# The first convolution of the recurrence between the sums of two norms and their broadcasts

## The chip, the cores and the metric

The kernel runs on one core of a Trainium2 chip. The metric is the device time of one launch in microseconds; the kernel before was run three times. The profile is one execution of the same program.

## What is computed

Four transformer layers over 256 tokens of width 1024. The change concerns the mixers of the last two layers (`_mixer` of the reference). Cut to what matters:

```python
proj = h @ w_in
c_q, c_kv, k_rope, q_m, k_m, v_m, o_m, i_m, f_m, g_mla, g_mlstm = split(proj)
q  = rmsnorm(c_q, q_norm_w) @ w_uq            # 384 -> 8 heads of 96
kv = rmsnorm(c_kv, kv_norm_w) @ w_ukv         # 256 -> 8 heads of 128
y_mla = attention(q, kv, rope(k_rope))
qk = silu(causal_dwconv(concat[q_m, k_m]))    # 4 taps, 1024 channels
y_mlstm = recurrence(qk, v_m, i_m, f_m) * sigmoid(o_m)
out = (sigmoid(g_mla) * (y_mla @ w_br_mla) + sigmoid(g_mlstm) * (y_mlstm @ w_br_mlstm)) @ w_out
```

`c_q` and `c_kv` are the low-rank activations and each has its own norm over its channels. `q_m` (the first 512 channels of `qk`) is what the code calls `conv(0)`.

## The kernel before

Activations lie with channels on the partitions and the 256 tokens along the free axis. Each float32 matrix product is done as three matmuls on halves of the operands: a high part (`wh`, `qH`, `hTh`) and the rest (`wl`, `qL`, `hTl`). So every weight piece of 128x1024 numbers is fetched by a DMA of SP's queue into a buffer `ws` (five), cast on ACT (L260) into `wh` and subtracted on DVE (L261) into `wl`; there are six pairs of `wh` and `wl`. `mm3` then issues the three matmuls (L275 to L277). Some fetches also draw a piece of the conditioning weights after or before them (`tick`), which cost a DMA (L498) and a product on DVE (L499).

The program is written as one long sequence. A scheduler of the framework then lays out each engine's queue: it plays the program through with its own costs, and an engine that is free takes, of the instructions whose operands and buffers are ready, the one that the program wrote first. Each engine then works through its queue in that fixed order. Buffers of one name (the banks `mm` and `acc` in PSUM, four each; `ws`, `wh`, `wl`, `nrm`) are handed out in the order of the program.

In `mixer2` the order of the program around the change is:

- the products `b1` and `b2` give `c_q`, `c_kv` and `k_rope`; copies L1361 to L1367 take them out of PSUM into `Fq`, `Fk`, `kr`
- `pgate`, 24 matmuls for the gates, from a small weight that GpSimd's queue fetches (L1371)
- `chan_norm` for `Fq` (three blocks), then for `Fk` (two): squares on ACT (L1193), sums over channels on TensorE (L1197, rows of the matmul are channels), the scale on DVE (L525) and the power -0.5 on GpSimd (L527), the broadcast over the partitions on TensorE (L554, into a bank `mm`), the product with the weight on DVE (L1201), and the split into `qH` and `qL`, or `vH` and `vL`, on ACT (L299) and DVE (L300)
- the product with `w_uq` in four groups of 18 matmuls, called uq below: own fetches (L1387), casts (L1390 to L1393), copies out (L1399, L1400)
- `conv(0)`: 96 matmuls into two banks `mm`, four activations (L1224), twelve taps on DVE (L1230), and one Silu over all four blocks (L1232)
- the gates' chain of small operations (L1406 to L1429), their transposes (L308), the product with `w_ukv` and the value product `pv` of the recurrence

Of the kernel before, what the change touches and what calls it, by code (L numbers as in the profile page):

```python
# [202 lines left out]
class Kern:  # L203
# [982 lines left out]
        nc.vector.tensor_copy(self.rot["q"][64:96], cs[64:96])  # L1186
        nc.vector.tensor_scalar(self.rot["q"][96:128], sn[96:128], C["sgn_q"][96:128], None, op0=ALU.mult)

    def chan_norm(self, F, n, count, w, H, L):

        nc = self.nc
        sq = self.scr((P, n, S))
        nc.scalar.activation(sq, F, AF.Square)  # L1193
        ps = self.bank("acc")
        for t in range(2):
            for k in range(n):
                nc.tensor.matmul(ps[:, t:t + 1], lhsT=sq[:, k, t * P:(t + 1) * P], rhs=self.one_col,  # L1197
                                 start=(t == 0 and k == 0), stop=(t == 1 and k == n - 1))
        v = self.bcast_rstd(ps[:, 0:2], count)
        for k in range(n):  # L1200
            nc.vector.scalar_tensor_tensor(F[:, k], F[:, k], w[:, k:k + 1], v, op0=ALU.mult, op1=ALU.mult)  # L1201
        self.split(H, L, F)


    def mixer2(self, i, mp, turn):
        nc, A, col = self.nc, self.A, self.col
# [12 lines left out]
        def conv(g):  # L1219
            bs = self.wstat(w_in, 672 + g * 512, 512, hT)  # L1220
            for b in range(2):
                for j in range(2):
                    c = g * 4 + b * 2 + j
                    nc.scalar.activation(mqk[:, c], bs[b][:, j], AF.Identity, bias=cb[:, c:c + 1], scale=cw[:, 24 + c:25 + c])  # L1224
                for j in range(2):
                    c = g * 4 + b * 2 + j
                    x, u = bs[b][:, j], mqk[:, c]
                    for tap in range(3):
                        sft = 3 - tap
                        nc.vector.scalar_tensor_tensor(u[:, sft:], x[:, :S - sft], cw[:, tap * 8 + c:tap * 8 + c + 1],  # L1230
                                                       u[:, sft:], op0=ALU.mult, op1=ALU.add)
            nc.scalar.activation(mqk[:, g * 4:g * 4 + 4], mqk[:, g * 4:g * 4 + 4], AF.Silu)  # L1232
# [126 lines left out]
        Fq, Fk = E4((P, 3, S)), E4((P, 2, S))  # L1359
# [16 lines left out]
        for k in range(KC):  # L1376
            self.mm3(pgate[:40, :S], (gh[:, k], gl[:, k]), (hT[0][:, k], hT[1][:, k]), k == 0, k == KC - 1)

        self.chan_norm(Fq, 3, 384, col["q_norm_w_2", i], qH, qL)
        self.chan_norm(Fk, 2, 256, col["kv_norm_w_2", i], vH, vL)  # L1380


        wu = A["w_uq_2"][i]
        for g in range(4):
# [9 lines left out]
            ps = self.bank("acc", (P, 2, S))  # L1394
# [3 lines left out]
                             hh == 0 and k == 0, hh == 1 and k == 2)  # L1398
            nc.scalar.copy(QH[:64, 2 * g:2 * g + 2], ps[:64])  # L1399
            nc.vector.tensor_tensor(QH[64:, 2 * g:2 * g + 2], ps[64:], self.rot["q"][64:, None, :].to_broadcast([64, 2, S]), ALU.mult)  # L1400
        conv(0)

        G, R = E4((8, 4, S)), E4((8, 4, S))
        ig, lf, Bc, Mx = G[:, 0], G[:, 1], G[:, 2], G[:, 3]
# [25 lines left out]
        ps = self.bank("acc", (P, 2, 4, 8))  # L1430
# [6 lines left out]
        ps = self.bank("acc", (P, 4, 4))  # L1437
# [9 lines left out]
        for g in range(2):  # L1447
            wh, wl = self.wload(A["w_ukv_2"][i].piece(0, g * 512), 2, 512)
            for b in range(2):
                ps = self.bank("acc", (P, 2, S))  # L1450
# [8 lines left out]
            ps = self.bank("acc", (P, 2, S))  # L1459
# [6 lines left out]
        ps = self.bank("acc", (P, 2, S))  # L1466
# [11 lines left out]
        for t in range(2):  # L1478
            v = T((P, 8, 65), f"vx{t}")
# [3 lines left out]
            w = E4((P, 8, 65))  # L1483
# [19 lines left out]
        for t in range(2):  # L1503
            ps = self.bank("acc", (P, 4, P))
# [208 lines left out]
```

## Time and profile before

| | us |
|---|---|
| median of 3 runs | 2158.03 (2157.88 to 2158.73) |
| the profiled execution | 2156.61 |
| its span | 2154.8 |

The span runs from the first to the last profiled instruction, so 1.81 us of the profiled execution lie around it. The two mixers in question lie at about 1300 to 1440 us and 1725 to 1870 us of the span.

### The profile page before, as it was taken

The page shows a single profiled execution, that of the slowest core. Times are in us where ns is not written, and L with a number is a line of the kernel's source. Part 1 is how long each engine was busy: PE and PEld are TensorE (multiplying, and loading weights), DVE is VectorE, ACT ScalarE, POOL GpSimd, SP SyncE. Part 2 cuts the span into 40 slices and gives each one's busy share as a digit, 9 for nine tenths or more (in the row PEclk, how much of TensorE's full clock was granted, in tenths as well). Part 3 has the DMA queues.
Part 4 walks back from the last instruction along what each step waited for, and adds up shares of the span by engine and source line. Part 5 has one row for each costly group of instructions (what it writes and reads, how often), then busy time and mean ns, then how long its engine had stood idle before and what let it go on. Part 6 is the DMA issues. An engine that isn't in the chain of part 4 may idle for free.

```text
span 2154.8 us, 36620 instructions
## 1 busy us (share of the span) xinstructions
PE 2064.4 (96%) x13990; PEld 1892.1 (88%) x13990; DVE 1811.5 (84%) x2593; ACT 1354.7 (63%) x1806; POOL 37.6 (2%) x49
## 2 busy tenths in 40 slices
PE   4999999989999999999999999999999999999998
PEld 4789999787888888888888888899999998989998
DVE  7888888987898999999898987967897878678765
ACT  3555445756878788778777775554655566447553
POOL 0000000000000000000000001000000000000000
PEclk9999999989999999999999999989999999899999
DMA  9768996788999989898999955646587656455662
GB/s 329 254 236 285 341 340 235 248 307 309 351 358 344 362 332 369 287 396 327 353 351 342 348 216 187 224 146 199 200 284 257 222 180 209 146 195 189 224 214 89
DMA packets 161305, 581.03 MB, mean 270 GB/s; under 512 B 17920, under 2 KB 20096, under 8 KB 161120
## 3 DMA queue, kind: packets, MB, share of 16 engines
q1 hardware_dynamic: 160256, 576.42, 74.5%
q8 instruction: 111, 1.82, 0.3%
q10 hardware_dynamic: 720, 1.73, 0.3%
q14 instruction: 74, 0.61, 0.1%
q0 software_dynamic: 144, 0.46, 0.1%
HBM read 577.49 MB, written 1.05 MB: 268 GB/s over the span
## 4 chain that ended last, share of the span: by engine, by line
PE 69%; DVE 4%; issue 2%; ACT 1%; DMA 1%; POOL 1%; DVEq 0%; POOLq 0%; ACTq 0%
PE mm L276 14%; PE mm L275 14%; PE mm L277 14%; PE acc L276 7%; PE acc L275 7%; PE acc L277 7%; DVE wl L261 1%; PE mm L979 1%; PE mm L308 1%; DMA ws<-in_ada_w_dram 1%; PE mm L990 1%; PE acc L308 1%; PE acc L1334 1%; PE acc L1280 1%; PE acc L1251 1%
## 5 line engine op out<-in xcount | busy, mean ns | idle before, releaser
L260 ACT CAST wh<-ws 128x1024 fp32r<-128x1024 f32 x525 | 546.6, 1051 | 421.5 <-PE mm L276 132.7
L261 DVE TENSOR_TENSOR wl<-ws,wh 128x1024 fp32r<-128x1024 f32 x525 | 631.5, 1221 | 102.9 <-ACT wh L260 99.0
L275 PE MATMUL mm<-hTh,wh 128*128 128x256 f32 x1536 | 435.7, 284 | 20.9 <-ACT wh L260 20.1
L277 PE MATMUL mm<-hTh,wl 128*128 128x256 f32 x1536 | 433.9, 283 | 5.3 <-DVE wl L261 5.3
L276 PE MATMUL mm<-hTl,wh 128*128 128x256 f32 x1536 | 434.1, 283 | 0.0
L275 PEld LDWEIGHTS mm<-hTh,wh 128*128 128x128 f32 x1536 | 293.8, 191 | 23.0 <-ACT wh L260 20.4
L277 PEld LDWEIGHTS mm<-hTh,wl 128*128 128x128 f32 x1536 | 293.1, 191 | 6.3 <-DVE wl L261 6.2
L276 PEld LDWEIGHTS mm<-hTl,wh 128*128 128x128 f32 x1536 | 296.9, 193 | 0.4
L275 PE MATMUL mm<-wh,x 128*128 128x512 f32 (+1 forms) x768 | 291.6, 380 | 0.0
L276 PE MATMUL mm<-wl,x 128*128 128x512 f32 (+1 forms) x768 | 288.2, 375 | 1.2 <-DVE wl L261 1.2
L277 PE MATMUL mm<-wh,x 128*128 128x512 f32 (+1 forms) x768 | 286.7, 373 | 0.0
L261 DVE TENSOR_TENSOR wl<-wx,wh 128x1024 fp32r<-128x1024 f32 x219 | 260.7, 1221 | 21.2 <-ACT wh L260 13.8
L499 DVE SCALAR_TENSOR_TENSOR ws<-ws,cb 128x1024 f32<-128x1024 f32 x190 | 230.7, 1220 | 51.0 <-DMA ws<-in_ada_w_dram 48.8
L260 ACT CAST wh<-wx 128x1024 fp32r<-128x1024 f32 x219 | 226.8, 1052 | 51.9 <-PE mm L277 26.2
L275 PE MATMUL acc<-y,wh 128*128 128x256 f32 x736 | 206.5, 283 | 6.5 <-ACT y L303 3.7
L276 PE MATMUL acc<-y,wh 128*128 128x256 f32 x736 | 207.2, 282 | 0.9 <-DVE y L304 0.9
L277 PE MATMUL acc<-y,wl 128*128 128x256 f32 x736 | 207.1, 282 | 0.7 <-DVE wl L261 0.7
L276 PEld LDWEIGHTS mm<-wl,x 128*128 128x128 f32 x768 | 145.6, 190 | 27.9 <-DVE wl L261 4.2
L277 PEld LDWEIGHTS mm<-wh,x 128*128 128x128 f32 x768 | 145.4, 189 | 25.9
L275 PEld LDWEIGHTS mm<-wh,x 128*128 128x128 f32 x768 | 145.5, 189 | 24.6 <-ACT nrm L1132 0.3
L261 DVE TENSOR_TENSOR wl<-y,wh 128x1024 fp32r<-128x1024 f32 x120 | 142.7, 1221 | 9.4 <-ACT wh L260 7.5
L275 PEld LDWEIGHTS acc<-y,wh 128*128 128x128 f32 x736 | 139.9, 191 | 7.3 <-ACT y L303 4.2
(442 smaller groups left out, 3743.0 us busy)
## 6 DMA issues: line engine op xcount, KB each, us to landing
wx<-in_moe_w_dram SPq DMA_DIRECT2D x219, 512.0 KB, 5.5
ws<-in_ada_w_dram SPq DMA_DIRECT2D x190, 512.0 KB, 4.8
ws<-in_moe_w_dram SPq DMA_DIRECT2D x159, 512.0 KB, 5.4
y<-in_moe_w_dram SPq DMA_DIRECT2D x120, 512.0 KB, 5.6
ws<-in_w_in_dram SPq DMA_DIRECT2D x116, 512.0 KB, 4.6
ws<-in_ffn_w_up_dram SPq DMA_DIRECT2D x88, 512.0 KB, 4.5
ws<-in_ffn_w_dram SPq DMA_DIRECT2D x66, 512.0 KB, 5.1
ws<-in_ffn_w_down_dram SPq DMA_DIRECT2D x44, 512.0 KB, 4.7
```

What stands on the lines that cost most here:

```text
L260: self.nc.scalar.copy(h, f)
L261: self.nc.vector.tensor_tensor(l, f, h, ALU.subtract)
L275: mm(out, lhsT=a[0], rhs=b[0], start=start, stop=False)
L276: mm(out, lhsT=a[0], rhs=b[1], start=False, stop=False)
L277: mm(out, lhsT=a[1], rhs=b[0], start=False, stop=stop)
L308: self.nc.tensor.transpose(out, in_, self.ident[:n, :n])
L499: nc.vector.scalar_tensor_tensor(f, f, 1.0, self.cb["c" + sfx], op0=ALU.mult, op1=ALU.mult, accum_out=m[:, k:k + 1])
L979: nc.tensor.matmul(ps[:, j], lhsT=part[:, t, cs], rhs=mr[:, t], start=(j == 0 and t == 0 and z == 0), stop=(j == 3 and t == 1 and z == 1))
L990: nc.tensor.matmul(ps[:, j], lhsT=part[:, cs], rhs=mT, start=(j == 0 and z == 0), stop=(j == 1 and z == len(parts) - 1))
L1251: nc.tensor.matmul(ps[:, j], lhsT=QH[:, h0 + j, t * P:(t + 1) * P], rhs=KH[:, h0 + j, :ek], start=(j == 0), stop=(j == hpb - 1))
L1280: nc.tensor.matmul(y[:, h], lhsT=pT[:, b * hpb + j, kb * P:(kb + 1) * P], rhs=V[:, kb, h * 64:(h + 1) * 64], start=(h == 0 and kb == 0), s ...
L1334: nc.tensor.matmul(pn[:, j], lhsT=W[:, q, j], rhs=vx[t][:, 2 * j + q], start=(j == 0), stop=(j == 3))
```

## The change

`chan_norm` is cut in two: `chan_sums` (squares and sums) and the rest. In `mixer2` both sums are written first, then `conv(0)`, then the rest of both norms. `conv(0)` is no longer written after uq.

```diff
-    def chan_norm(self, F, n, count, w, H, L):
+    def chan_sums(self, F, n):
...
-        v = self.bcast_rstd(ps[:, 0:2], count)
+        return ps[:, 0:2]
+
+    def chan_norm(self, F, n, sums, count, w, H, L):
+
+        nc = self.nc
+        v = self.bcast_rstd(sums, count)
...
-        self.chan_norm(Fq, 3, 384, col["q_norm_w_2", i], qH, qL)
-        self.chan_norm(Fk, 2, 256, col["kv_norm_w_2", i], vH, vL)
+        sums = [self.chan_sums(Fq, 3), self.chan_sums(Fk, 2)]
+        conv(0)
+        self.chan_norm(Fq, 3, sums[0], 384, col["q_norm_w_2", i], qH, qL)
+        self.chan_norm(Fk, 2, sums[1], 256, col["kv_norm_w_2", i], vH, vL)
...
-        conv(0)
 
         G, R = E4((8, 4, S)), E4((8, 4, S))
```

## Rows read from the trace of the kernel before

**Rows 1.** The page's first part: busy time, share of the span, instructions.

```profile
PE 2064.4 (96%) x13990; PEld 1892.1 (88%) x13990; DVE 1811.5 (84%) x2593; ACT 1354.7 (63%) x1806; POOL 37.6 (2%) x49
```

**Rows 2.** Groups of PE's instructions, 1325.93 to 1353.12: busy, mean ns, idle before.

```profile
L275 PE MATMUL acc<-y,wh 128*128 128x256 f32 x24 | 6.3, 276 | 0.0
...
L1197 PE MATMUL acc<-cst,nrm 128*128 128x1 f32 x20 | 2.4, 251 | 0.9 <-ACT nrm L1193 0.9
L554 PE MATMUL mm<-cst,rstd 128*128 128x128 f32 x8 | 1.9, 381 | 1.2 <-POOL rstd L527 1.2
```

**Rows 3.** The same groups in the second mixer, 1750.84 to 1779.97.

```profile
L554 PE MATMUL mm<-cst,rstd 128*128 128x128 f32 x8 | 2.1, 409 | 3.8 <-POOL rstd L527 3.8
```

**Rows 4.** Timeline of PE, first mixer: start, duration, instruction, [idle before, releaser].

```profile
1326.85 2.39 PE L1197 MATMUL acc<-cst,nrm 128*128 128x1 f32 x20 [0.92 <-ACT nrm L1193]
...
1331.19 1.22 PE L554 MATMUL mm<-cst,rstd 128*128 128x128 f32 x4 [1.05 <-POOL rstd L527]
...
1363.30 0.50 PE L276 MATMUL mm<-wl,hTh 128*128 128x512 f32 x1 [1.08 <-DVE wl L261]
```

**Rows 5.** Timeline of PE, second mixer.

```profile
1750.68 1.39 PE L1197 MATMUL acc<-cst,nrm 128*128 128x1 f32 x12
1753.19 0.89 PE L554 MATMUL mm<-cst,rstd 128*128 128x128 f32 x4 [1.12 <-POOL rstd L527]
...
1758.23 1.22 PE L554 MATMUL mm<-cst,rstd 128*128 128x128 f32 x4 [2.64 <-POOL rstd L527]
...
1759.89 0.41 PE L275 MATMUL mm<-hTh,wh 128*128 128x256 f32 x1
1760.10 0.41 PE L276 MATMUL mm<-hTl,wh 128*128 128x256 f32 x1
...
1764.01 0.28 PE L276 MATMUL acc<-y,wh 128*128 128x256 f32 x1
...
1764.58 0.28 PE L275 MATMUL acc<-y,wh 128*128 128x256 f32 x1
```

**Rows 6.** Stretches: length, busy of PE, PEld, DVE, ACT, POOL, PE's clock, DMA, GB/s.

```profile
1330.00:1332.00 2.00, 0.95 (x6) 0.81 (x5) 1.76 (x4) 1.97 (x3) 1.14 (x1) 0.58 0.94 340
1336.00:1338.00 2.00, 2.00 (x15) 2.00 (x14) 0.00 (x0) 0.66 (x1) 0.00 (x0) 0.71 0.55 211
...
1762.00:1764.00 2.00, 2.00 (x12) 2.00 (x11) 1.93 (x4) 0.00 (x0) 0.00 (x0) 0.54 0.00 0
```

**Rows 7.** Timeline of ACT, first mixer.

```profile
1332.89 0.81 ACT L299 CAST y<-nrm 128x768 fp32r<-128x768 f32 x1
...
1353.12 1.94 ACT L1224 ACTIVATE e<-mm,tab 128x256 f32<-128x256 f32 x4 [1.05 <-PE mm L277]
...
1362.05 1.28 ACT L1232 ACT_TABLE_LOAD   x1 [0.48 <-DVE mst L1421]
1363.34 1.06 ACT L1232 ACTIVATE e<-e 128x1024 f32<-128x1024 f32 x1
```

**Rows 8.** Timeline of ACT, second mixer.

```profile
1779.97 1.93 ACT L1224 ACTIVATE e<-mm,tab 128x256 f32<-128x256 f32 x4 [1.10 <-PE mm L277]
```

**Rows 9.** Timeline of DVE, both mixers.

```profile
1330.50 1.26 DVE L1201 SCALAR_TENSOR_TENSOR nrm<-nrm,tab,mm 128x256 f32<-128x256 f32 x3
...
1334.38 0.95 DVE L300 TENSOR_TENSOR y<-nrm,y 128x768 fp32r<-128x768 f32 x1
...
1356.97 4.38 DVE L1230 SCALAR_TENSOR_TENSOR e<-mm,tab,e 128x253 f32<-128x253 f32 x11
...
1749.04 1.23 DVE L261 TENSOR_TENSOR wl<-ws,wh 128x1024 fp32r<-128x1024 f32 x1 [0.25 <-ACT wh L260]
```

**Rows 10.** SP's queue in the first mixer, and its issues from 1310 to 1330.

```profile
1315.40 3.70 SPq L1387 DMA_DIRECT2D ws<-in_w_uq_dram  x4
1319.83 0.33 SPq L252 DMA_DIRECT2D ws<-in_w_in_dram  x1
...
ws<-in_w_in_dram SPq DMA_DIRECT2D x4, 512.0 KB, 5.2
```

## The prediction

> **What bounds the kernel now.** First the page: PE is busy for 96% of the span [rows 1], so the time moves when PE stands still or runs slowly, and a DVE at 84% is near enough to count where PE waits for it. Then PE's groups and its timeline in the two stretches that the change touches. Each runs from the end of `pgate` to the last matmul of uq and `conv(0)`: in the first mixer from 1325.93 (the sums start at 1326.85 after 0.92 idle) to the activations L1224 at 1353.12 [rows 4, 7], so 27.2 us; in the second from 1750.68 to 1779.97 [rows 5, 8], so 29.3 us. In both PE ends with the same work done: 20 passes of sums, 8 of broadcasts, 96 matmuls of `conv(0)`, 72 of uq (the three groups of uq hold 24 each [rows 2]).
>
> Inside them PE waits 0.9 for the squares and 1.2 for the powers of GpSimd in the first [rows 2], and 3.8 for the powers in the second [rows 3, 5]. The clock follows: granted 0.58 in 1330 to 1332, still 0.71 in 1336 to 1338, and in the second mixer 0.54 in 1762 to 1764 [rows 6]. A matmul then steps 0.21 us (1759.89 to 1760.10) where it steps 0.115 at full clock (1764.01 to 1764.58 is five steps) [rows 5], that is the 1.2 GHz level in place of 2.4. At full clock without waits a stretch would need 2.4 for the sums, 1.2 for the broadcasts and 168 x 0.115 = 19.3, together 22.9. So 4.3 and 6.4 us are lost, 10.7 in all or 0.5% of the run: the most that the change can win here.
>
> The order is worth seeing. `conv(0)` is written after uq, but in the trace its first matmuls follow the broadcasts directly (1759.89 are `mm<-hTh,wh`), because uq needs `qH`. It already hides the chain from broadcast to `qL`. It doesn't fill the wait ahead of the broadcasts: in the second mixer the first weight piece was split at 1750.27 [rows 9], yet PE stood idle until 1753.19 [rows 5]. What it lacked was its two `mm` banks, handed out in the order of the program, behind those of the broadcasts. That reading is mine; the trace shows only the idle PE beside a finished piece.
>
> **The change part by part.** *The wait ahead of the broadcasts goes.* `conv(0)` now gets its banks first, and its four pieces are fetched where uq's were, from 1315.40 on, landing after about 5.2 [rows 10]; three of the four should be split before `pgate` ends. So PE goes from the sums into 96 matmuls with no gap. Gain: the 1.2 and 3.8 us of waiting, and the slow clock that follows them.
>
> *Another wait takes its place.* A free engine takes what was written first. While `conv(0)`'s matmuls are ready, the broadcasts stand behind them. Call E the end of `conv(0)`. First mixer: 0.5 (the wait for the squares, between 0 and 0.9, or up to 2 more if the third piece's cast stands ahead of the copy L1366 and its DMA is late) + 2.4 + 96 x 0.115 = 11.0, so E is 13.9 after the start. Second: 2.4 + 11.0 = 13.4.
>
> After E the chain for uq is: broadcast, three products L1201 of 1.26, cast L299 of 0.81, and L300 of 0.95 for the second matmul [rows 7, 9]. But the outputs of `conv(0)` are written ahead of it. The first bank closes 6 matmuls, 0.7 us, before E; its first activation takes half of a us (four in 1.94 [rows 7]), so DVE starts the taps at about E, before the first broadcast is out. Twelve taps at 4.38/11 = 0.40 make 4.8, then L1201: 6.1 after E. On ACT the Silu becomes ready at 4.8, ahead of the cast, with a table load of 1.28 and 1.06 of work [rows 7]: free at 7.3, so `qH` at 8.1 and uq from E + 8.2. Behind the waiting L554 on PE's queue stand uq, then the gates' transposes, `w_ukv` and `pv`.
>
> Could PE do something else? The six `wh` buffers are then held by uq's four groups and the two pieces of `w_ukv`, which waits for `vH`; `pv`, which filled PE at this place before, gets its first buffer only when uq's first group is done. I find no filler, so PE stands for about 7 us after the second broadcast (E + 1.2). The broadcasts themselves cost nothing: they lie under the taps.
>
> *The slow clock moves with the hole.* In the trace PE needed about 5 us of matmuls at half clock (1332 to 1337, 1759 to 1764 [rows 5, 6]) to get full clock back. The same after a hole of 7 us: 5 us that do the work of 2.6, so 2.4 lost. I take it once per mixer, as before; a second fall already in the sums would add 2.4 each, none at all takes 2.4 off. uq: 72 x 0.115 = 8.3, + 2.4. It ends at E + 18.9.
>
> Sums: first mixer 13.9 + 18.9 = 32.8 against 27.2, +5.6. Second 13.4 + 18.9 = 32.3 against 29.3, +3.0.
>
> *What comes later.* Before, the taps came while `pv`'s pieces were to be split: L261 stood behind them on DVE and PE waited 1.08 at 1363.30 [rows 4, 9]. With the taps gone from there, I take 1.1 off; bounds 0 and 1.4.
>
> *DMAs and queues.* Four fetches of 512 KB, with those of the conditioning weights drawn by them, pass uq's four on SP's queue. uq's land some 10 us later than now, near 1330; uq needs them at E + 8, near 1348. That cover of 18 us hides it; without it each late group would cost its landing. GpSimd's queue keeps its order. DVE is the doubt: splits, conditioning products and the gates' chain now compete with uq's splits during `conv(0)`; if the taps start late, uq slips by as much. I bound that by 0 and 2 us a mixer and take 0.
>
> Total +5.6 + 3.0 - 1.1 = +7.5. The profiled execution goes from 2156.61 to 2164.1, and the median, 1.4 above it, to about 2165.5.
>
> *A rule weighed.* In the trace the Silu starts 0.01 us after its table load ends, and the load takes 1.28 [rows 7]. The Trainium skill, "ScalarE: Activation LUTs", section "What ACT_TABLE_LOAD costs", puts a drain of about 1.38 us beside the load, 2.66 for each switch of tables. By that rule the cast would come 1.4 later in each mixer, +10.3 in all and 2168.3; by the row it is +7.5. The trace shows no such drain and I go by it. The table switch itself is not new, only its place on the path is.
>
> **The rivals.** *The broadcasts slip into the product* (faster). If PE is given L554 at least 32 matmuls before E, the 3.7 us from broadcast to `qL` are hidden and the stretch falls to 23.4 and 22.9: -3.8 and -6.4, with the later 1.1 it is 2147; halfway, 2152. For it: the trace has PE's order mixed freely wherever something wasn't ready. Against: it needs `conv(0)` to run dry, and its pieces come early. With the slow clock, uq has to start on average less than 4.4 us after E for any gain at all.
>
> *The products come before the taps.* Then uq starts at about E + 3.0, which makes -2 to +0.4 and -4.6 to -2.2, in all about -3 to -8: 2150 to 2155. Against: the taps are ready first and twelve of them follow each other without a gap.
>
> *Nothing changes*, because the queues come out as before: 2158. Against: the banks and the fetches change places.
>
> *A drain at the table*, as above: 2168.3, from the same chain with 1.4 more per mixer.
>
> **How the numbers follow.** The forecast has 0.65; its own range is 2161 (the cast gets ahead of the Silu, -2.6, and a little more) to 2173 (both bounds of DVE, a late square, one more fall of the clock). Slipped broadcasts 0.17, products first 0.08, nothing 0.05, the drain 0.05. About 0.2%, or 4.3 us, is what a measurement can tell from no change. Slower: 0.58 of the forecast and the drain, 0.63. Same: 0.07 of the forecast's low edge, the 0.05, and 0.06 from the two faster rivals, 0.18. Faster 0.19. A range of 2152 to 2173 leaves out the full slip (0.1) and the outermost of the forecast.
>
> **What would show it.** Right: in PE's timeline the 20 passes of sums, then some 96 `mm` matmuls at 0.115, then both L554, then an idle PE of 5 us or more until the first `acc<-y,wh`; L1201 on DVE after ten or more L1230; L299 behind the Silu; a granted clock near 0.5 in the first us of uq. Wrong: L554 amid `conv(0)`, uq within 4 us of the last `mm`, or `pv` in the hole, which would say that the buffers go to whoever is ready.

## The result, and the profile after

| | before | after |
|---|---|---|
| median, us | 2158.38 (2157.88 to 2159.27, 4 runs) | 2179.22 (2177.9 to 2185.97, 4 runs) |
| span of the profiled execution, us | 2154.8 | 2176.1 |

The ratio is 1.0116, with a 95% interval of 1.0092 to 1.014: the change costs 20.8 us. The forecast had the sign (slower, 0.63), but 2165.5 and a range that ended at 2173. Lines of the kernel after stand 5 to 7 further down (taps L1235, activations L1229, Silu L1237, product of the norms L1206, values of the attention L1285). The page's first part shows the work unchanged: PE is busy about as long and in the same number of matmuls as in [rows 1], in a longer span.

```profile
PE 2071.1 (95%) x13990; PEld 1898.5 (87%) x13990; DVE 1814.8 (83%) x2593; ACT 1353.4 (62%) x1805; POOL 36.3 (2%) x49
```

PE's timeline of the kernel after, first mixer and then (1786 on) the second; it answers to [rows 4, 5]:

```profile
1331.29 2.39 PE L1197 MATMUL acc<-cst,nrm 128*128 128x1 f32 x20 [1.34 <-ACT nrm L1193]
...
1346.46 1.05 PE L554 MATMUL mm<-cst,rstd 128*128 128x128 f32 x8
1355.23 1.22 PE L275 MATMUL acc<-y,wh 128*128 128x256 f32 x4 [7.71 <-ACT y L299]
...
1406.29 1.97 PE L1285 MATMUL acc<-nrm,nrm 128*128 128x64 f32 x8 [2.72 <-DVE nrm L1280]
...
1786.06 1.22 PE L275 MATMUL acc<-y,wh 128*128 128x256 f32 x4 [7.62 <-ACT y L299]
...
1836.42 1.97 PE L1285 MATMUL acc<-nrm,nrm 128*128 128x64 f32 x8 [2.33 <-DVE nrm L1280]
```

The wait for the powers is gone, as meant. In its place PE stands 7.7 and 7.6 us ahead of uq, which was forecast, and 2.7 and 2.3 us ahead of the values of the attention, some 50 us later, which was not. In the kernel before, PE reached those values (L1280 there) without a wait in the first mixer and after 0.52 in the second:

```profile
1393.01 2.00 PE L1280 MATMUL acc<-nrm,nrm 128*128 128x64 f32 x16
...
1817.56 2.00 PE L1280 MATMUL acc<-nrm,nrm 128*128 128x64 f32 x16 [0.52 <-DVE nrm L1275]
```

DVE's timeline of the first mixer shows what each of the two waits for:

```profile
1348.59 0.15 DVE L1427 TENSOR_TENSOR mst<-nrm 8x1 f32<-8x1 f32 x1
1348.77 0.48 DVE L1235 SCALAR_TENSOR_TENSOR e<-mm,tab,e 128x253 f32<-128x253 f32 x1
1349.16 0.47 DVE L1206 SCALAR_TENSOR_TENSOR nrm<-nrm,tab,mm 128x256 f32<-128x256 f32 x1
1349.55 3.59 DVE L1235 SCALAR_TENSOR_TENSOR e<-mm,tab,e 128x254 f32<-128x254 f32 x9
1353.06 0.47 DVE L1206 SCALAR_TENSOR_TENSOR nrm<-nrm,tab,mm 128x256 f32<-128x256 f32 x1
1353.45 0.47 DVE L1235 SCALAR_TENSOR_TENSOR e<-mm,tab,e 128x254 f32<-128x254 f32 x1
1353.84 0.47 DVE L1206 SCALAR_TENSOR_TENSOR nrm<-nrm,tab,mm 128x256 f32<-128x256 f32 x1
1354.23 0.47 DVE L1235 SCALAR_TENSOR_TENSOR e<-mm,tab,e 128x255 f32<-128x255 f32 x1
1354.62 0.86 DVE L1206 SCALAR_TENSOR_TENSOR nrm<-nrm,tab,mm 128x256 f32<-128x256 f32 x2
...
1398.17 3.50 DVE L261 TENSOR_TENSOR wl<-ws,wh 128x1024 fp32r<-128x1024 f32 x3 [0.73 <-ACT wh L260]
1404.02 1.23 DVE L499 SCALAR_TENSOR_TENSOR ws<-ws,cb 128x1024 f32<-128x1024 f32 x1 [2.35 <-DMA ws<-in_ada_w_dram]
...
1405.16 0.48 DVE L1235 SCALAR_TENSOR_TENSOR e<-mm,tab,e 128x253 f32<-128x253 f32 x1
1405.56 0.68 DVE L1280 COPY nrm<-acc 128x512 f32<-128x512 f32 x1
```

The taps stand between the products, as forecast, and they start 2.15 us after the last matmul of `conv(0)` (1346.62), because the gates' chain and an L261 come first. In the second place a conditioning product, L499, stands idle for 2.35 us until its fetch lands, and the copy L1280 that PE needs is queued behind it. The second mixer has the same wait:

```profile
1834.14 1.22 DVE L499 SCALAR_TENSOR_TENSOR ws<-ws,cb 128x1024 f32<-128x1024 f32 x1 [2.29 <-DMA ws<-in_ada_w_dram]
```

In the second mixer of the kernel before this place on DVE reads:

```profile
1813.02 3.50 DVE L261 TENSOR_TENSOR wl<-ws,wh 128x1024 fp32r<-128x1024 f32 x3 [0.73 <-ACT wh L260]
1816.43 0.48 DVE L1230 SCALAR_TENSOR_TENSOR e<-mm,tab,e 128x253 f32<-128x253 f32 x1
1816.82 0.68 DVE L1275 COPY nrm<-acc 128x512 f32<-128x512 f32 x1
```

No L499 stands between the third L261 and the copy. SP's queue of the kernel after shows that the fetch of the first mixer was issued at 1399.43, so 4.6 us passed until the product could start:

```profile
1395.36 1.54 SPq L252 DMA_DIRECT2D ws<-in_w_in_dram  x2
1399.43 0.33 SPq L498 DMA_DIRECT2D ws<-in_ada_w_dram  x1
```

ACT's timeline of the kernel after, first mixer, answers to [rows 7]:

```profile
1345.96 1.94 ACT L1229 ACTIVATE e<-mm,tab 128x256 f32<-128x256 f32 x4 [1.18 <-PE mm L277]
...
1354.34 0.83 ACT L299 CAST y<-nrm 128x768 fp32r<-128x768 f32 x1 [5.52 <-DVE nrm L1206]
1355.19 1.28 ACT L1237 ACT_TABLE_LOAD   x1
1356.48 1.06 ACT L1237 ACTIVATE e<-e 128x1024 f32<-128x1024 f32 x1
```

The cast went ahead of the Silu, not behind it. The stretches of PE's clock (columns as in [rows 6], the clock is the third from the end):

```profile
1334.00:1336.00 2.00, 2.00 (x14) 2.00 (x13) 1.93 (x3) 2.00 (x5) 0.70 (x1) 0.61 0.53 148
...
1350.00:1355.00 5.00, 0.00 (x0) 0.00 (x0) 5.00 (x14) 0.66 (x1) 0.00 (x0) 0.65 0.14 57
1355.00:1361.00 6.00, 5.77 (x25) 5.52 (x26) 5.85 (x14) 3.80 (x5) 0.00 (x0) 0.50 0.25 87
...
1406.00:1408.00 2.00, 1.71 (x8) 1.71 (x9) 2.00 (x6) 0.00 (x0) 0.00 (x0) 0.53 0.92 266
1408.00:1410.00 2.00, 2.00 (x11) 2.00 (x11) 1.74 (x5) 0.00 (x0) 0.00 (x0) 0.50 0.08 31
```

Each of the three waits of the first mixer (1.3 for the squares, 7.7, 2.7) is followed by matmuls at the 1.2 GHz level; a mean above 0.50 has some at 2.4 GHz in it.

**Where the time went.** Three marks on PE, from the traces: the end of `pgate`; the last matmul of uq and `conv(0)` (the stretch lies between these two; here it runs to that matmul's own end, where the prediction stopped at the start of the activations, 0.6 us earlier); and the last matmul of the recurrence's states, 10 to 13 us behind the last of the attention's values. In the first mixers before and after it is in these rows:

```profile
1428.12 1.54 PE L1515 MATMUL acc<-nrm,nrm 64*64 64x65 f32 x32
```

```profile
1446.03 1.54 PE L1521 MATMUL acc<-nrm,nrm 64*64 64x65 f32 x32
```

Between the marks PE has the same matmuls to do in all five profiles, except that in the second mixer of the kernel after five more stand ahead of the last mark, about 0.6 us at full clock.

| us, first / second mixer | stretch | from there to the last state | both |
|---|---|---|---|
| before | 27.8 / 29.8 | 75.9 / 75.8 | 103.7 / 105.5 |
| before, once more | 28.4 / 29.2 | 75.9 / 74.8 | 104.4 / 104.0 |
| after | 36.9 / 33.4 | 80.7 / 79.5 | 117.6 / 112.8 |
| after, second profile | 35.1 / 33.3 | 81.3 / 78.3 | 116.3 / 111.7 |
| after, third profile | 36.6 / 34.8 | 83.9 / 79.1 | 120.5 / 114.0 |

The stretches cost 9.1 + 3.6 = 12.7, the part behind them 4.8 + 3.7 = 8.5; together 21.2, against 20.8 of the medians. That these agree so closely is partly luck: the other pairs of rows make 18.8 to 26.1. Up to the first `pgate` the two profiles differ by 4.0 us (1325.93 and 1329.95); further profiles of the changed kernel have it at 1324.1 and 1321.7, so that is no effect of the change.

### The profile page after: what moved, and what is told of

Same layout as the page of the kernel before. It is cut to its first block, busy times and chain, and to the rows that moved or that the text cites. A ratio compares the mean times of both kernels' runs of the same rounds, so it can differ in the third digit from the quotient of the medians.

```text
span 2176.1 us, 36622 instructions
## 1 busy us (share of the span) xinstructions
PE 2071.1 (95%) x13990; PEld 1898.5 (87%) x13990; DVE 1814.8 (83%) x2593; ACT 1353.4 (62%) x1805; POOL 36.3 (2%) x49
## 4 chain that ended last, share of the span: by engine, by line
PE 66%; DVE 4%; ACT 2%; DMA 2%; issue 2%; POOL 0%; DVEq 0%; POOLq 0%; ACTq 0%
PE mm L276 13%; PE mm L275 13%; PE mm L277 13%; PE acc L276 7%; PE acc L275 7%; PE acc L277 7%; DVE wl L261 1%; DMA ws<-in_ada_w_dram 1%; PE mm L979 1%; PE mm L308 1%; ACT wh L260 1%; PE mm L990 1%; PE acc L1285 1%; DVE ws L499 1%; PE acc L308 1%
## 5 line engine op out<-in xcount | busy, mean ns | idle before, releaser
L261 DVE TENSOR_TENSOR wl<-ws,wh 128x1024 fp32r<-128x1024 f32 x525 | 631.4, 1220 | 116.1 <-ACT wh L260 111.4
L261 DVE TENSOR_TENSOR wl<-wx,wh 128x1024 fp32r<-128x1024 f32 x219 | 260.6, 1220 | 21.1 <-ACT wh L260 13.8
L499 DVE SCALAR_TENSOR_TENSOR ws<-ws,cb 128x1024 f32<-128x1024 f32 x190 | 230.6, 1219 | 56.6 <-DMA ws<-in_ada_w_dram 54.9
L275 PE MATMUL acc<-y,wh 128*128 128x256 f32 x736 | 209.6, 288 | 22.3 <-ACT y L299 15.3
L276 PE MATMUL acc<-y,wh 128*128 128x256 f32 x736 | 210.4, 286 | 2.0 <-DVE y L304 2.0
L261 DVE TENSOR_TENSOR wl<-y,wh 128x1024 fp32r<-128x1024 f32 x120 | 142.6, 1220 | 9.4 <-ACT wh L260 7.5
```

The source lines that it names most:

```text
L261: self.nc.vector.tensor_tensor(l, f, h, ALU.subtract)
L275: mm(out, lhsT=a[0], rhs=b[0], start=start, stop=False)
L276: mm(out, lhsT=a[0], rhs=b[1], start=False, stop=False)
L499: nc.vector.scalar_tensor_tensor(f, f, 1.0, self.cb["c" + sfx], op0=ALU.mult, op1=ALU.mult, accum_out=m[:, k:k + 1])
```

## The experiments

All ratios are to the kernel before on the same chip. On those chips single runs of the kernel before spread from about 2143 to 2163 us, so small differences are read from 4 to 12 runs of a version beside 23 to 29 of the kernel before, and from where the profile shows waits. In the kernels whose `conv` is cut up the lines shift again (taps L1247 or L1248, copy for the values of the attention L1296 or L1297).

**The changed kernel again, one execution.**

> The changed kernel once more, for its trace. If the slower time sits in the two mixers alone, PE's first sums of the first mixer start within 1 us of where they started in the kernel before (1326.85) or drift by a different amount than the 4.4 us of the first trace (1331.29); if the change also costs time upstream, the same 4 us come again. In both cases a hole of 7 to 8 us stands after the broadcasts in each mixer, and the span is 2172 to 2177.

Measured: 2170.78 (span 2169.0; before 2153.64 in the median of 29 runs). Waits ahead of uq of 7.94 and 7.62, ahead of the values of 3.27 and 1.51. What was read above repeats, though the span is 3 us under the expected range; the kernel before is 4.7 us faster on this chip too.

**Only the taps behind the norms.** The activations, taps and Silu are written behind both norms; the 96 matmuls stay ahead of the broadcasts. For this `conv` is cut into its banks and pieces, its matmuls (by blocks of 128 channels of the input, KC is 8), and the rest.

```diff
-        conv(0)
+        cv = conv_begin(0)
+        conv_mm(cv, KC)
         self.chan_norm(Fq, 3, sums[0], 384, col["q_norm_w_2", i], qH, qL)
         self.chan_norm(Fk, 2, sums[1], 256, col["kv_norm_w_2", i], vH, vL)
+        conv_end(0, cv)
```

> The matmuls of the first convolution stay between the sums and the broadcasts, its activations, taps and Silu are written after both norms. Theory one (the hole after the broadcasts is made by the taps standing ahead of the products L1201 on DVE): the hole shrinks from 7.7 to 2 to 4 us in each mixer, the clock falls less, and the time is 2163 to 2170. Theory two (the earlier fetches of the convolution's weights and what they push back make the time): the fetches are as in the changed kernel, so the time stays at 2175 or more.

Measured: 1.0023 (1.0002 to 1.0045), with a median of 2160.16, where the first theory had 2163 to 2170. The rows are PE's and DVE's, first mixer:

```profile
1343.09 1.22 PE L275 MATMUL acc<-y,wh 128*128 128x256 f32 x4 [4.04 <-ACT y L299]
```

```profile
1340.52 0.48 DVE L1248 SCALAR_TENSOR_TENSOR e<-mm,tab,e 128x253 f32<-128x253 f32 x1
1340.92 2.03 DVE L1206 SCALAR_TENSOR_TENSOR nrm<-nrm,tab,mm 128x256 f32<-128x256 f32 x5
```

All five products now run after one tap, and the hole is 4.0 (3.8 in the second mixer) instead of 7.7. What is left of it is the chain itself: broadcast, products, cast, uncovered because the matmuls that could cover it are done. The stretches are 30.5 and 30.3. Ahead of the values there is no wait in the first mixer and one of 2.77 in the second.

**Half of the matmuls behind the broadcasts.**

```diff
-        conv(0)
+        cv = conv_begin(0)
+        conv_mm(cv, 4)
...
+        conv_mm(cv, 4)
+        conv_end(0, cv)
```

> Half of the convolution's matmuls stand between the sums and the broadcasts, then both norms are written, then the other half and the taps. The fetches are in the order of the changed kernel. Theory one: the broadcasts run in the middle of the product, their chain is hidden under the second half, no hole is left and no slow clock, and the time is 2146 to 2154, under both kernels. Theory two: 2170 or more.

Measured: 1.0001 (0.9984 to 1.0018). The stretches, to the end of uq, are 25.3 and 22.6, with no hole. What they gain is lost behind them: from there to the last state it takes 81.8 and 78.2. PE's row of the first mixer (3.2 in the second):

```profile
1354.20 0.79 PE L276 MATMUL mm<-wl,hTh 128*128 128x512 f32 x1 [2.70 <-DVE wl L261]
```

The split of `pv`'s first piece stands behind the taps on DVE.

**Both broadcasts ahead of the convolution.** The powers and broadcasts of both norms are written before `conv(0)`, the products behind it.

> Sums, both broadcasts, then the whole convolution, then the products and splits of the norms, uq last. The wait for the powers ahead of the broadcasts is back, the hole is not, as the products L1201 find DVE free under the convolution. Theory one: 2154 to 2162, about as before. Theory two (moving the convolution and its fetches ahead of uq costs by itself): 2170 or more.

Measured: 1.0053 (1.0034 to 1.0072), with stretches of 26.1 and 27.4. The expectation failed: the stretches were shorter than before the change, and the kernel was slower. Its waits lie behind: 2.94 ahead of `pv`, and 1.15 and 3.58 ahead of the values of the attention. This run first said that the hole was not the whole loss.

**The taps left out.** The changed kernel without the twelve taps (the three shifted terms of the first convolution are not computed).

```diff
-                    for tap in range(3):
+                    for tap in range(3 if g else 0):
```

> The order of the changed kernel with the twelve taps of the first convolution left out in both mixers (its three shifted products are not computed; activations and Silu stay). If the hole ahead of uq is the twelve taps standing ahead of the norms' products on VectorE: the products follow the broadcasts directly, the hole falls from 7.6 to 7.9 us to 3 to 4 in each mixer, the stretches from 33 to 37 us to 28 to 32, and the time falls by 8 to 10 us against the changed kernel, to a ratio of 1.005 to 1.008 against the kernel before. If the hole is the split that follows the products (cast on ScalarE behind other work): the hole stays above 6 and the ratio above 1.009. If most of the loss lies later (values of the attention, its copies), the hole shrinks but the ratio stays above 1.009.

Measured: 1.0104 (1.0068 to 1.014). PE's rows of the first mixer, then ACT's:

```profile
1351.39 1.22 PE L275 MATMUL acc<-y,wh 128*128 128x256 f32 x4 [4.47 <-ACT y L299]
1354.21 0.58 PE L276 MATMUL acc<-y,wh 128*128 128x256 f32 x1 [1.60 <-DVE y L300]
```

```profile
1348.27 1.28 ACT L1250 ACT_TABLE_LOAD   x1
1349.56 1.06 ACT L1250 ACTIVATE e<-e 128x1024 f32<-128x1024 f32 x1
1350.52 1.33 ACT L299 CAST y<-nrm 128x768 fp32r<-128x768 f32 x2
```

Without taps the Silu is ready early, and now its table load and its work do stand ahead of the cast, 2.3 us, just as the prediction had them. With a second wait of 1.6 for L300 the hole is 6.1 in all, 5.2 in the second mixer, and the stretches are 35.6 and 30.3. And the late waits are there as before, 2.53 and 2.45: DVE's load of taps is not what makes them. The last of the three readings came nearest: a smaller hole and yet a ratio above 1.009. The time is not measurably below that of the changed kernel.

**The change in the first mixer only.**

> The change in the first of the two mixers only, the second as before. If the loss belongs to the change and not to chance: the first mixer's stretch is 35 to 37 us (27 before), the second's 29 to 30, gaps of 1.5 to 3.5 us at the values of the attention in the first mixer only, and about 60% of the whole loss remains, a ratio of 1.006 to 1.008. If the excess of the first mixer over the forecast (9.8 us where 5.6 were forecast) was chance of one profile: stretch 32 to 33, ratio 1.002 to 1.004.

Measured: 1.0075 (1.0053 to 1.0097). The stretches are 36.4 and 30.1, the late waits 2.96 and 0.76, the times to the last state 118.5 and 106.2. So hole and late wait belong to the change, and the excess in the first mixer is not chance.

**Half of the matmuls as late as before; only the taps late.** Two orders: in the first, 48 matmuls stand between sums and broadcasts, and the other 48, the activations, the taps and the Silu follow uq. In the second the halves stand around the norms, and the activations, taps and Silu follow uq.

> Two pieces of the first convolution's product (48 matmuls) between the sums and the broadcasts; then the norms and uq; the other two pieces and the activations, taps and Silu behind uq, as before the change. If the wait ahead of the broadcasts was real and the loss is the taps' place: no wait for the power, no hole above 1 us before uq, the taps as late as before, so the stretches are 23 to 25 us (27.2 and 29.3 before), the late gaps are as before (about 1 us), ratio 0.995 to 0.998. If the uncovered chain from broadcast to the split operand needs more than what is left of the convolution: a hole of 1 to 3 us, ratio 0.999 to 1.002. If every move of the convolution ahead of uq costs later (as where both broadcasts came first): stretches of 23 to 25, but a ratio of 1.000 to 1.005.

> Half of the first convolution's product, both norms, the other half; uq; and only then the activations, taps and Silu. It differs from the run with the halves around the norms only in the place of the taps. If the gap of 2.7 to 3.2 us before the recurrence's value product came from taps ahead of its splits: that gap falls to 1 us or less, ratio 0.995 to 0.999. If it came from the order of the fetches (uq's behind all four pieces): the gap stays at 2 to 3 us, ratio about 1.000.

Measured: 1.0041 (1.0019 to 1.0062) and 1.0072 (1.0046 to 1.0098). The first has stretches without a hole (0.9 and 0.7 of waiting), but in the first mixer waits of 1.19 and 0.72 right behind uq and a late one of 2.55 ahead of the values: the third reading of its expectation, by which every move of the convolution costs later. The second refutes both of its readings: with the taps behind uq the wait ahead of `pv` grew in the first mixer, and in the second PE waits 4.29 for the gates' transposes instead. PE's row of the first mixer:

```profile
1361.57 0.80 PE L276 MATMUL mm<-wl,hTh 128*128 128x512 f32 x1 [4.71 <-DVE wl L261]
```

On DVE ten taps and four products of uq's outputs run from 1352.60 to 1360.31, while `pv`'s piece, cast on ACT from 1357.58 after 1.31 of waiting for its fetch, is ready from 1358.6 on. In the first mixers of these orders something that PE wants soon stands behind the 4.8 us of taps; before the change they fell where only 1.08 was lost. It need not be so: the second mixers of the halves with the hold, below, have no wait of more than 0.4 us up to the last state.

**The conditioning fetches held back.** From the product with `w_ukv` to the second half of the attention's gate no conditioning weights are fetched; the rest of the mixer makes up for it at twice the rate.

```diff
+        rate, self.rate = self.rate, 0
         V = E4((P, 2, 512))
         for g in range(2):
...
         gate_mla(1)
+        self.rate = 2 * rate
```

Once on the changed kernel, once on the kernel before, and on the order with halves around the norms; with them a further profile of the kernel before.

> The changed kernel, in which no piece of the conditioning weights is fetched from the product with w_ukv to the second half of the gate of the attention; they are made up at twice the rate in the rest of the mixer. If the late waits (2.7 and 2.3 us before the values of the attention, with the slow clock behind them) come from conditioning products that wait for their fetch on VectorE ahead of the copy of the attention's weights: both gaps fall below 1 us, the holes of 7.7 stay, and the ratio falls from 1.0116 to 1.006 to 1.008. If those waits come from the splits and taps that are late themselves: gaps of 1.5 to 3 us stay, ratio 1.010 to 1.013. If the making up costs elsewhere: no late gap, but waits for fetches behind the gate of the attention and a ratio above 1.010.

> The kernel before with the same hold of the conditioning fetches. It is the base for the changed kernel with the hold: the difference of the two is the stretch alone. If the hold is free by itself: ratio 0.998 to 1.001 and late gaps of at most 0.5 us. If the making up costs: 1.002 to 1.005. By the theory of the hole the changed kernel with the hold is then 13 us (the lost time inside the stretches: 9.7 of waiting and 3.4 of slow clock) above this one, 0.6%; by the rival (the loss is spread over later waits that any shift brings) less than 6 us.

> The convolution's product in two halves around the broadcasts, the taps before uq, and the hold of the conditioning fetches. If the gap of 2.7 to 3.2 us ahead of the recurrence's value product came from VectorE's load: two conditioning products of 1.2 us less stand in it, the gap falls to 1 to 2 us, and the ratio is 0.994 to 0.998. If it is the taps alone: gap as before, ratio 0.998 to 1.001. If the hold costs elsewhere: above 1.001.

> The kernel before once more, for its profile on this chip. If single profiles repeat: stretches of 27 to 28 and 29 to 30 us, late gaps of at most 1.1 us, and the end of pgate within 4 us of 1325.9. If what was read as an effect of the change is chance: late gaps of 2 us or more before the values of the attention here too.

Measured: changed kernel with the hold 1.0045 (1.0026 to 1.0064); kernel before with the hold 1.0001 (0.9983 to 1.0019); halves with the hold 0.9975 (0.9958 to 0.9993). The changed kernel with the hold, PE's and then DVE's rows of the first mixer:

```profile
1349.63 1.23 PE L275 MATMUL acc<-y,wh 128*128 128x256 f32 x4 [8.15 <-ACT y L299]
...
1397.13 1.55 PE L1285 MATMUL acc<-nrm,nrm 128*128 128x64 f32 x12
```

```profile
1395.99 0.48 DVE L1235 SCALAR_TENSOR_TENSOR e<-mm,tab,e 128x253 f32<-128x253 f32 x1 [0.85 <-ACT e L1229]
1396.39 0.68 DVE L1280 COPY nrm<-acc 128x512 f32<-128x512 f32 x1
```

The hole is there (8.15, and 6.48 in the second mixer), the late wait is gone in both, and with it the slow clock behind it: from the stretch to the last state it is 74.8 and 74.7 where the changed kernel needs 80.7 and 79.5, at mean clocks of 1.00 and 1.00 in place of 0.94 and 0.96. The ratio fell below the expected 1.006 to 1.008. Over the whole path to the last state, with the same matmuls in it, the two kernels with the hold differ by 110.7 - 105.6 = 5.1 and 107.5 - 104.1 = 3.4, together 8.5 us; their medians (2163.77 and 2155.57) differ by 8.2, between the 13 and the less than 6 of the expectation. The sum hides that the parts differ the other way round: the stretches by 9.1 and 4.7, what follows by -4.0 and -1.3, since the kernel before with the hold had mean clocks of 0.96 and 0.98 there, without a wait of more than 0.4 us. The halves with the hold still wait 2.78 ahead of `pv` in the first mixer, so there the hold did not do what its first reading said. The further profile of the kernel before has no wait ahead of the first mixer's values and one of 0.84 in the second (0.52 in the first profile).

**The size, on one chip.** The changed kernel and the ones with the hold timed together, and the hold begun before the sums already.

> The changed kernel once more, timed beside the changed kernel with the hold. If the first measurement (1.0116) holds here too: 1.010 to 1.013. If a part of it belonged to that chip: 1.007 to 1.010, as the single execution of 2170.8 against 2153.6 suggested. Profile: holes of 7.5 to 8, late gaps of 1.5 to 3.3 us, lost time (waiting and slow clock) in the first 116 us of both mixers near 40 us.

> The changed kernel with the hold of the conditioning fetches, on the same chip as the changed kernel. If the late waits make a good part of the loss: 0.3 to 0.7% below the changed kernel. If the first result was the chip's: less than 0.2% below it.

> Halves around the broadcasts, taps before uq, hold. If it is faster than the kernel before: 0.996 to 0.9985 again. If that was chance: 0.999 to 1.002.

> As the run with halves and hold, with the hold begun before the sums, so that two more fetches of conditioning weights and their products leave VectorE in the stretch. If VectorE's load there is what leaves the gap of 2.8 us ahead of the recurrence's value product in the first mixer: gap below 1.5 us, 0.1 to 0.2% below the run with the hold begun after uq. If the gap comes from the taps alone: gap as before, same time.

Measured: changed kernel 1.009 (1.0058 to 1.0122), with the hold 1.0049 (1.0029 to 1.0068); medians 2174.98 and 2162.82, 12.2 us apart (by the ratios, 0.41%, it is 8.8, so the size is rough). Whether a part of the first 1.0116 belonged to its chip, the interval does not tell. Halves with the hold: 0.9991 (0.9968 to 1.0014), so the 0.9975 of the first time is not confirmed, and no version here is shown to beat the kernel before by more than the 0.2% that can be told. With the early hold: 1.0012 (0.9988 to 1.0036), and the wait ahead of `pv` is 2.24 where it was 2.76: the conditioning products that it takes away are not what makes that one.

## Why the prediction was wrong, point by point

**The wait ahead of the broadcasts goes: right.** No wait for the powers is left in either stretch.

**Another wait takes its place: right in place, in size partly by luck.** From the end of `conv(0)` to uq the forecast had 8.2; measured are 1355.23 - 1346.62 = 8.6 and 1786.06 - 1777.55 = 8.5. Its working was not right in detail. DVE was late by 2.15 us, where the sum took 0 (its bounds were 0 and 2). The Silu, 2.34 us with its table load, stood behind the cast and not ahead of it: two of the cast's three products ran among the last taps, and it could start at 1354.34, before the last tap was done. The two errors nearly cancel. (4.8 + 1.28 + 1.06 is also 7.1, not the 7.3 of the prediction.) No filler came, and the broadcasts were over at 1347.51, before the first tap, so they cost nothing, though not because they lay under the taps.

**The slow clock moves with the hole: right, somewhat small.** uq took 11.7 and 11.3 us against 8.3 + 2.4 = 10.7.

**The bounds that were left at their likely value.** In the first mixer the squares kept PE waiting 1.34 (taken 0.5), and the clock fell already right behind the sums (0.61 in 1334 to 1336), which the prediction had as a bound of +2.4. So `conv(0)` ended 16.7 after the start, not 13.9. In the second mixer, without that wait, it was 13.5 against 13.4. The stretches came to +9.1 and +3.6 against +5.6 and +3.0. Of this forecast 0.6 and 0.5 were a wrong reading of the kernel before: its activations, where the prediction ended the stretch, start 0.6 ahead of the last matmul, and the second stretch was begun 0.2 early.

**What comes later: the step that failed.** The prediction took 1.1 off, "bounds 0 and 1.4", as if nothing behind the stretch could get worse. Measured is +8.5 there. The wait of 1.08 ahead of `pv` did go; but the step on DMAs and queues followed the fetches of uq past the four of `conv(0)`, which were indeed covered, and had the conditioning weights "drawn by them" in a subordinate clause. Where their products would then stand on DVE it didn't ask beyond `conv(0)`. With the new order one of them came to stand ahead of the copy of the attention's weights, waiting for a fetch that had just been issued. That costs 2.7 and 2.3 of waiting instead of none and 0.5, and the slow clock that follows. With the measured stretches in its sum, the prediction would have come to 2165.5 + 4.1 = 2169.6, inside its range; it is the part behind them that took the time out of it.

The hold shows it: it takes these waits away, costs nothing that could be measured by itself (1.0001), and takes 12.2 us off the median of the changed kernel on the same chip. With it the change costs 0.45 to 0.49%, 9.0 and 10.7 us between the medians. The stretches then still cost 11 to 12 us where the sum had 8.6, and the part behind them takes about as long as before the change.

The hold doesn't separate the one product that waits from the others that it removes from that place as well. All eighteen profiles together do. Of their 36 mixers 15 have a wait of more than 1 us ahead of the values (1.15 to 3.58), and in each of the 15 an L499 ahead of the copy has waited 1.1 to 2.7 us for its fetch. In the other 21, where PE waits at most 0.84, none has. In some of these an L499 stands at the same place but didn't wait for its fetch; this is the second mixer of the run with half of the matmuls behind uq, where PE waited 0.18:

```profile
1817.26 1.22 DVE L499 SCALAR_TENSOR_TENSOR ws<-ws,cb 128x1024 f32<-128x1024 f32 x1
```

So it is the wait for the fetch, and not the product's work; that the taps left out changed nothing in the late waits says the same of DVE's load. Why the framework's scheduler put that product there wasn't tried.

**The rivals.** The broadcasts didn't slip into the product, and the products didn't pass the taps; of the five products one ran after the first tap, the others late among the taps or behind them. The drain is out too: the table load begins 0.02 us after the cast ends and the Silu 0.01 us after the load ends. The Trainium skill, "ScalarE: Activation LUTs", section "What ACT_TABLE_LOAD costs", puts a drain of about 1.38 us beside the load; the measured rows show none, here as in [rows 7].

## What to carry to other kernels

A matmul block that is moved into a wait takes its followers along: the place of its vector work in the queue decides more than the filled wait, and a block that already covered another chain can't cover two. When an order is written for a scheduler, follow everything that the moved step draws, background fetches too, to the place where their consumers land on the vector engine, over the whole layer and not only to the end of the stretch. Where background work can be held back in a tight part at no cost, as here, doing so takes such waits away.

## What was not expected of the hardware

The same program runs at different granted clocks in different executions, without a difference in its waits. From the recurrence's last state matmul to the next sums, first mixer, two profiles of the kernel before (the windows' columns are as in [rows 6]):

```profile
1429.60:1523.80 94.20, 91.17 (x750) 89.39 (x749) 65.86 (x109) 40.20 (x53) 3.27 (x2) 0.91 0.54 179
```

```profile
1425.80:1512.90 87.10, 83.68 (x749) 81.95 (x749) 65.43 (x109) 40.04 (x53) 3.27 (x2) 1.00 0.58 193
```

PE stands still for 3.0 and 3.4 us in them, and yet one takes 7.1 us longer, at a mean clock of 0.91 instead of 1.00. The whole spans are 2154.8 and 2142.0. On one chip, too, runs of this kernel went from 2142.94 at a mean clock of 0.982 to 2160.47 at 0.974. Nor does every fall follow a wait. In the second mixer of the last run of halves with the hold PE has no wait of more than 0.4 us up to the last state, and yet there is this stretch, with PE busy throughout at a clock of 0.50:

```profile
1836.00:1842.00 6.00, 6.00 (x32) 5.74 (x31) 4.57 (x14) 1.54 (x2) 0.00 (x0) 0.50 0.69 247
```

A single profile therefore says where waits are, but not what a change of some microseconds is worth; the loss up to the last state could be read only because most falls of the clock there follow waits, and only to the few microseconds by which its profiles differ.
